# Batched 64x64 matmul: a gate before the second a tile's loads, its transposes behind the first multiplication, and two result blocks of every other tile for VectorE

## The chip, the cores and the metric

One core of one Trainium2 chip. The time is the device time of a launch in us; where several runs were made, the median is given. Every timed run used here was in the fast state; the state of the two kernels of transfers, run once each, is unknown.

A ratio is the mean time of one kernel's fast runs over that of the kernel before in the same rounds on the same chip, so it is not quite the ratio of the medians quoted beside it.

## The reference

```python
def setup_inputs():
    return {"a": np.random.randn(1024, 64, 64).astype(np.float32),
            "b": np.random.randn(1024, 64, 64).astype(np.float32)}

def reference(a, b):
    return np.matmul(a, b).astype(np.float32)
```

Each of a, b and the output is 16.78 MB. The program must read 33.55 MB and write 16.78 MB; there is little arithmetic.

## The kernel before

a is worked on in 8 tiles (s) of 128 batches, b and the result in 16 tiles (t) of 64 batches. A tile of a after the first comes as three quarters that GpSimd's DMA casts to bf16 on the way, and one plain fp32 quarter from ScalarE's queue. It is regrouped, transposed on TensorE as packed pairs of bf16, copied from PSUM by ScalarE, and spread by VectorE into block-diagonal weights. b comes plain on the queues of SyncE and ScalarE in turn and is cast on chip. Results leave PSUM in eight blocks per tile and go out through GpSimd's queue.

b is read in runs of `u n` = 128 fp32 (512 bytes), plain quarters of a in runs of `v k` = 1024 fp32 (4 KB), and results are written in runs of `w n` = 256 fp32 (1 KB).

```python
    a_v = a.rearrange("(s g h) (mp v) k -> s h g mp (v k)", h=4, g=32, v=16)
    b_v = b.rearrange("(t g h) (kp u) n -> t (h kp) g (u n)", h=4, g=16, u=2)
    o_v = out.rearrange("(t gh x) (mo w) n -> t (x mo) gh (w n)", gh=8, x=8, w=4)
    ...
    def load_a(s):
        a_sb = a_pool.tile([128, 3, 16, 64], bf16, name="a_sb")
        for h in range(3):
            nc.gpsimd.dma_start(                     # casts fp32 to bf16
                out=a_sb[:, h, :, :].rearrange("p v k -> p (v k)"), in_=a_v[s, h])
        a_raw = a_pool.tile([128, 16, 64], fp32, name="a_raw")
        nc.scalar.dma_start(out=a_raw[:]..., in_=a_v[s, 3])

    def load_b(t):
        b_sb = b_pool.tile([128, 16, 128], fp32, name="b_sb")
        queue = nc.scalar if t % 2 else nc.sync
        queue.dma_start(out=b_sb[:], in_=b_v[t])
    ...
    # stores, in multiply(t)
            nc.gpsimd.dma_start(out=o_v[t, :, lo : lo + n, :], in_=o_sb[:, lo : lo + n]...)
    ...
    with tc.manual_schedule():
        load_first_a()                               # plain, SyncE and ScalarE
        for t in range(3):
            load_b(t)
        ... # memsets, load_a(1), load_a(2) on GpSimd without a wait
        regroup(0); transpose(0, 0); transpose(0, 1)
        load_b(3); spread(0); cast(0)
        regroup(1); load_a(A_AHEAD); transpose(1, 0)
        for t in range(n_t):
            ... # spread(t+1), cast(t+1), load_b(t+4), load_a, multiply(t),
            ... # regroup(s+2), transposes, store(t-1)
```

(Cut; calls on one line are joined here.)

## Time and profile before

| | before |
|---|---|
| time, median of the first 3 runs (lowest, highest) | 135.2 us (134.85, 135.22) |
| span of the profiled run | 133.2 us |
| VectorE, ScalarE busy | 96.3, 86.8 us |
| first multiplication starts | 25.9 us |
| b0 landed, last b (b15) landed | 19.8, 113.7 us |
| last result copy ends, last store landed | 128.2, 131.7 us |

The prediction shows how these are read. One thing to keep in mind: GB/s in these views counts the written side, so a casting load counts half of what it reads.

### The profile page before, as it was taken

Reading aid. Unit: us, or ns where it says so; the run is one execution under the profiler, and the core shown is the slowest. Engines: PE = TensorE matmul, PEld = TensorE weight load, DVE = VectorE, ACT = ScalarE, POOL = GpSimd, SP = SyncE. Lnnn points to the kernel's source line nnn. Section 1 sums busy time; section 2 is a strip of 40 time slices with the busy share of each in tenths; the row PEclk is TensorE's granted clock in tenths of the full one; section 3 lists DMA queues with packets and bytes.
Section 4 is the critical chain, followed back from the end, with each engine's and each line's share of the span. In section 5 each row is a group of like instructions: output and inputs, shape, how many; then the busy total and the mean of one; then the engine's idle time right before and its main releaser. Section 6 shows DMA issues by size and latency. Waiting matters only on the chain.

```text
span 133.2 us, 2835 instructions
## 1 busy us (share of the span) xinstructions
PE 67.9 (51%) x1152; PEld 62.6 (47%) x1152; DVE 96.3 (72%) x121; ACT 86.8 (65%) x160; POOL 35.9 (27%) x49
## 2 busy tenths in 40 slices
PE   0000900784539259486358637951996195269300
PEld 0000900784439257475257527941995094268200
DVE  5920064943999249996999899799969996897740
ACT  3105525089950699489939992998399759969910
POOL 8981004000802017112413302030203020322460
PEclk9999995589965865579977985698569959955955
DMA  3999999999999999999999999999999999999893
GB/s 75 365 335 310 308 308 328 318 304 306 314 328 341 389 321 318 336 400 386 367 307 294 394 404 387 323 302 335 399 394 396 387 397 402 400 404 388 298 320 133
DMA packets 17485, 45.01 MB, mean 338 GB/s; under 512 B 1088, under 2 KB 1088, under 8 KB 17472
## 3 DMA queue, kind: packets, MB, share of 16 engines
q0 software_dynamic: 7440, 22.28, 54.7%
q10 hardware_dynamic: 5520, 13.11, 25.6%
q1 hardware_dynamic: 4512, 9.44, 20.1%
q8 instruction: 9, 0.15, 0.4%
q14 instruction: 4, 0.03, 0.1%
HBM read 33.55 MB, written 16.78 MB: 378 GB/s over the span
## 4 chain that ended last, share of the span: by engine, by line
DVE 29%; ACT 18%; PE 15%; DMA 13%; issue 10%; ACTq 7%; POOL 3%; SPq 1%; POOLq 1%; DVEq 0%
ACT o_sb L172 16%; DVE at_bd L128 14%; PE o_ps L184 13%; DMA b_sb<-in_b_dram 13%; DVE b_bf L139 6%; ACTq L72 4%; DVE o_sb L172 4%; POOL out_dram L161 3%; ACTq L91 3%; DVE a_bf L106 3%; PE at_ps L115 2%; DVE a_bf L103 2%; ACT b_bf L139 1%; SPq L85 1%; POOLq L274 1%
## 5 line engine op out<-in xcount | busy, mean ns | idle before, releaser
L172 ACT COPY o_sb<-o_ps 64x512 f32<-64x512 f32 x105 | 60.9, 580 | 20.3 <-PE o_ps L184 13.1
L184 PEld LDWEIGHTS <-at_bd 128*128 128x128 bf16 x1024 | 43.9, 115 | 35.5 <-DVE b_bf L139 25.1
L184 PE MATMUL o_ps<-b_bf,at_bd 128*128 128x64 bf16 x960 | 43.7, 218 | 31.2 <-DVE b_bf L139 22.4
L128 DVE COPY at_bd<-at_sb 32x1024 f32<-32x1024 f32 x64 | 45.6, 713 | 9.5 <-ACT at_sb L118 7.7
L161 POOL DMA_DIRECT2D out_dram<-o_sb x20 | 19.4, 968 | 77.9 <-DVE o_sb L172 72.5
L115 PE MATMUL at_ps<-identity,a_bf 128*128 128x128 f32 x128 | 23.3, 344 | 25.0 <-ACT a_bf L100 13.3
L115 PEld LDWEIGHTS at_ps<-identity,a_bf 128*128 128x128 f32 x128 | 19.3, 181 | 26.1 <-issue 20.8
L118 ACT COPY at_sb<-at_ps 128x512 f32<-128x512 f32 x32 | 17.4, 588 | 7.7 <-PE at_ps L115 7.3
L172 DVE COPY o_sb<-o_ps 64x512 f32<-64x512 f32 x15 | 10.4, 695 | 15.4 <-ACT o_sb L172 15.2
L139 DVE CAST b_bf<-b_sb 128x2048 bf16<-128x2048 f32 x14 | 17.4, 1245 | 0.4
L68 POOL DMA_DIRECT2D a_sb<-in_a_dram x21 | 12.5, 609 | 14.7 <-DVE a_bf L103 9.5
L106 DVE CAST a_bf<-a_raw 128x1024 bf16<-128x1024 f32 x7 | 7.0, 1003 | 1.9 <-DMA a_raw<-in_a_dram 1.9
L103 DVE COPY a_bf<-a_sb 128x3072 bf16<-128x3072 bf16 x7 | 6.7, 960 | 0.2
L100 ACT CAST a_bf<-o_sb 128x1024 bf16<-128x1024 f32 x2 | 2.0, 1042 | 7.4 <-issue 7.4
L100 DVE CAST a_bf<-o_sb 128x1024 bf16<-128x1024 f32 x2 | 2.5, 1228 | 2.6 <-DMA o_sb<-in_a_dram 2.6
L212 DVE MEMSET at_bd<- 128x4096 f32 x1 | 3.5, 3472 | 0.8 <-issue 0.8
L172 DVE COPY o_sb<-at_ps 64x256 f32<-64x256 f32 x8 | 3.4, 422 | 0.1
L139 ACT CAST b_bf<-b_sb 128x2048 bf16<-128x2048 f32 x1 | 1.9, 1898 | 2.3 <-DMA b_sb<-in_b_dram 2.3
L172 ACT COPY o_sb<-at_ps 64x256 f32<-64x256 f32 x8 | 2.9, 366 | 0.1
L209 ACT ACT_TABLE_LOAD x1 | 1.3, 1283 | 2.3 <-issue 2.3
L184 PE MATMUL at_ps<-b_bf,at_bd 128*128 128x64 bf16 x64 | 2.6, 212 | 0.3 <-DVE at_bd L128 0.3
L216 POOL MEMSET at_bd<- 128x2048 f32 x1 | 1.9, 1851 | 0.0
(12 smaller groups left out, 5.3 us busy)
## 6 DMA issues: line engine op xcount, KB each, us to landing
out_dram<-o_sb POOLq DMA_DIRECT2D x14, 1024.0 KB, 21.4
a_sb<-in_a_dram POOLq DMA_DIRECT2D x21, 256.0 KB, 19.7
a_raw<-in_a_dram ACTq DMA_DIRECT2D x7, 512.0 KB, 16.5
o_sb<-in_a_dram ACTq DMA_DIRECT2D x2, 512.0 KB, 7.3
o_sb<-in_a_dram SPq DMA_DIRECT2D x2, 512.0 KB, 6.4
out_dram<-o_sb POOLq DMA_DIRECT2D x2, 512.0 KB, 4.8
out_dram<-o_sb POOLq DMA_DIRECT2D x4, 256.0 KB, 3.7
b_sb<-in_b_dram SPq DMA_DIRECT2D x8, 0.5 KB, 16.8
```

The lines of the kernel that those rows point to most:

```text
L68: nc.gpsimd.dma_start(out=a_sb[:, h, :, :].rearrange("p v k -> p (v k)"), in_=a_v[s, h])
L72: nc.scalar.dma_start(out=a_raw[:].rearrange("p v k -> p (v k)"), in_=a_v[s, 3])
L100: copy(a_bf[:, :, h, :], a_sb[h].rearrange("p (v k) -> p v k", v=16))
L103: nc.vector.tensor_copy(a_bf[:, :, 0:3, :], cast_sb[:].rearrange("p h v k -> p v h k"))
L106: nc.vector.tensor_copy(a_bf[:, :, 3, :], raw[:])
L115: nc.tensor.transpose(at_ps[:, vo, :], a_cols[:, 4 * vo + 2 * j + wl, :], identity[:])
L118: nc.scalar.copy(at_tiles[s][:, j, :, wl, :, :], at_ps[:].rearrange("p vo (g mp) -> p g mp vo", mp=4),)
L128: nc.vector.tensor_copy(bd[rows, :, :, :, h, :].rearrange("p j g wl mo -> p j (g wl) mo"), at_tiles[t // 2][rows, :, half, :, :, :].rearrange(
L139: (nc.vector.tensor_copy if t else nc.scalar.copy)(b_bf[:], b_sb[:])
L161: nc.gpsimd.dma_start(out=o_v[t, :, lo : lo + n, :], in_=o_sb[:, lo : lo + n].rearrange("p gh j wl n -> p (gh j wl n)"),)
L172: copies[2 * par + wl](dst, src)
L184: nc.tensor.matmul(o_ps[:, gl, g % 2, j, :], at_bd[:, j, g, :, u], b_bf[:, g, 64 * u : 64 * u + 64], start=(u == 0), stop=(u == 1),)
```

## The change

Its intent: let b0, which the first multiplication needs, land without the casting loads of later a tiles in its way; let the first multiplication start without waiting for tile 1; and take VectorE's wait for ScalarE out of the even tiles.

```diff
@@ result blocks, in multiply(t)
                 copies = [nc.scalar.copy] * 4
-                if half:
-                    copies[3] = nc.vector.tensor_copy
+                if half and t % 2:
+                    copies[2:] = [nc.vector.tensor_copy] * 2
@@ before the loop
-        nc.gpsimd.memset(bd_tiles[1][:, 0], 0.0)
-        load_a(1)
-        nc.gpsimd.memset(bd_tiles[1][:, 1], 0.0)
-        for s in range(2, A_AHEAD):
+        nc.gpsimd.memset(bd_tiles[1][:], 0.0)
+        nc.gpsimd.tensor_copy(gate[:], a_tiles[0][3][:, 0:1])
+        for s in range(1, A_AHEAD):
             load_a(s)
...
-        regroup(1)
-        load_a(A_AHEAD)
-        transpose(1, 0)
@@ in the loop
-            if half == 0:
-                if s + 1 + A_AHEAD < n_s:
-                    load_a(s + 1 + A_AHEAD)
+            if half == 0 and 0 < s < n_s - 1 - A_AHEAD:
+                load_a(s + 1 + A_AHEAD)
             multiply(t)
-            if half == 0 and s + 2 < n_s:
+            if t == 0:
+                regroup(1)
+                load_a(A_AHEAD)
+                load_a(A_AHEAD + 1)
+                transpose(1, 0)
+            elif t == 1:
+                regroup(2)
+            elif half == 0 and s + 2 < n_s:
                 regroup(s + 2)
```

(The declaration of `gate` is left out.)

More of the change, by code (lines that the diff above doesn't have):

```diff
@@ L60 @@
     warm = consts.tile([128, 2], fp32)
+    gate = consts.tile([128, 1], fp32)
     a_tiles, b_tiles, abf_tiles, at_tiles, bbf_tiles = {}, {}, {}, {}, {}
```

## The prediction

> **What bounds the kernel now.** I read the page first. Its engine shares point at VectorE (72% busy), and its chain of waits is a mixture of VectorE, ScalarE and PE. Both mislead. The DMA row says that the 16 engines are full from the second slice to the last but one:
>
> ```profile
> span 133.2 us, 2835 instructions
> DVE  5920064943999249996999899799969996897740
> ACT  3105525089950699489939992998399759969910
> DMA  3999999999999999999999999999999999999893
> HBM read 33.55 MB, written 16.78 MB: 378 GB/s over the span
> ```
>
> To see whether "full" means "can do no more", I asked for busy time by stretch (columns: window, length, busy time of each engine, clock, DMA share, GB/s).
>
> ```profile
> 2.00:4.00 2.00, 0.00 (x0) 0.00 (x0) 2.00 (x1) 1.48 (x3) 2.00 (x3) 1.00 0.86 209
> 4.00:7.00 3.00, 0.00 (x0) 0.00 (x0) 2.79 (x2) 0.00 (x0) 3.00 (x4) 1.00 1.01 399
> 100.00:120.00 20.00, 10.92 (x217) 10.11 (x217) 17.98 (x23) 16.08 (x30) 4.24 (x4) 0.82 1.03 398
> 120.00:125.00 5.00, 4.07 (x91) 3.79 (x88) 3.36 (x7) 4.87 (x10) 0.83 (x2) 0.70 1.00 374
> 125.00:130.00 5.00, 0.00 (x0) 0.00 (x0) 3.04 (x8) 1.88 (x6) 3.53 (x5) 0.65 0.85 293
> ```
>
> A share stays above 1 only while queues are full (packets of several queues overlap on an engine). It is below 1 in two places: the first 4 us, and after 120 us, where the rate falls from 398 to 374 and 293 GB/s although stores are still to come.
>
> Next I priced the traffic, from DMA views of short windows (queue, packets, MB, share). The first line is the whole of 115 to 120 us, where only stores run. The next three are 102 to 110 us, stores with b. The last three are 10 to 15 us, casting loads of a (q0) beside two queues of b and plain a.
>
> ```profile
> q0 software_dynamic: 522, 2.01, 101.9%
> ...
> q0 software_dynamic: 469, 1.81, 58.7%
> q10 hardware_dynamic: 393, 0.80, 26.8%
> q1 hardware_dynamic: 267, 0.51, 16.9%
> ...
> q0 software_dynamic: 261, 0.47, 49.8%
> q1 hardware_dynamic: 261, 0.53, 30.9%
> q10 hardware_dynamic: 261, 0.53, 27.4%
> ```
>
> Stores: 2.01 MB in 5 us, 401 GB/s. b: in 8 us, 1.81 MB of stores take 4.5 us at that rate, so 1.33 MB of b (the window's 3.14 MB less the stores) go in 3.5 us, 381 GB/s. Casts: the two hardware queues' 1.07 MB take 2.8 us at that rate, so 0.47 MB written take the other 2.2 us, 215 GB/s of bf16 written. Plain a: 399 GB/s from the 4-to-7 us row. Now the whole program: stores 16.78 MB / 401 = 41.8 us; b 16.78 / 381 = 44.0; plain a, 11 loads of 0.524 MB, 5.77 / 399 = 14.5; casts, 21 loads of 0.262 MB, 5.51 / 215 = 25.6; instruction fetches about 0.6. Sum **126.5 us of full-rate DMA** in a span of 133.2. The rest is 6.7 us: 2.1 us before the first packet and about 1.0 in the half-filled start (2 to 4 us at 209 of 399 GB/s), some 1.8 from the last packet (131.4) to the end of the span, and the remaining 1.8 almost all after 120 us. Between 4 and 120 us nothing is lost.
>
> The tail of the issue list shows why the end is thin: the last stores land 3.3 to 7.0 us after issue, against a median of 17 over the kernel, so from tile 13 on the queue holds little and each store waits for its copies.
>
> ```profile
> 118.81 0.89 POOL L161 DMA_DIRECT2D out_dram<-o_sb  x1 [3.50 <-DVE o_sb L172]
> 122.42 0.76 POOL L161 DMA_DIRECT2D out_dram<-o_sb  x1 [2.72 <-ACT o_sb L172]
> 124.93 1.50 POOL L161 DMA_DIRECT2D out_dram<-o_sb  x2 [1.75 <-DVE o_sb L172]
> 128.45 0.72 POOL L161 DMA_DIRECT2D out_dram<-o_sb  x1 [0.34 <-DVE o_sb L172]
> ```
>
> So computation matters only in that it must finish early enough for the last stores to queue behind one another. It finishes at 127.7 us (last result copy) now, and at 25.9 us begins its first multiplication:
>
> ```profile
> 11.21 1.99 ACT L100 CAST a_bf<-o_sb 128x1024 bf16<-128x1024 f32 x2 [7.41 <-issue]
> 17.60 2.83 DVE L128 COPY at_bd<-at_sb 32x1024 f32<-32x1024 f32 x4 [7.33 <-ACT at_sb L118]
> 19.84 1.90 ACT L139 CAST b_bf<-b_sb 128x2048 bf16<-128x2048 f32 x1 [2.27 <-DMA b_sb<-in_b_dram]
> 25.88 0.32 PE L184 MATMUL o_ps<-b_bf,at_bd 128*128 128x64 bf16 x2
> ```
>
> **What the Trainium skill says.** "DMA: Bandwidth & Descriptors", section "Queues, rings and completion order", has each engine go round-robin between its queues by packet. The trace agrees: 261, 261 and 261 packets of three queues in 10 to 15 us. So a casting load holds b0 back even though it was issued later. The same page, section "Issuing engines are not separate DMA queues", says that DMAs of all issuers share the same 16 engines. That is why holding one queue back reorders the traffic and does not shorten it; the flat loss from 4 to 120 us agrees. The same page's "Specifications" gives about 358 GB/s of HBM per core; here stores run at 401, so the measurement decides. "VectorE: DVE Perf Modes", section "The TRN2 errata", has a PSUM copy cost VectorE 120 + FD cycles at 0.96 GHz and ScalarE 172 + FD at 1.2 GHz, 658 and 570 ns for 512 columns; the trace has 695 and 580.
>
> **The change, part by part.**
>
> *The gate.* GpSimd copies one column of the first a tile's last quarter before it issues the six casting loads of tiles 1 and 2 (and three of tile 3, next in its stream). That quarter lands at 9.99 us now. The casts put their first packets on at 7.1 us; without them in the way, I estimate 9.0 to 9.3. The first cast now took 3.5 us from the end of its issue to its first packet, so casts start near 12.7 us. From 9.0 to 12.7, b0 and b1 share the engines: 3.7 us at 381 GB/s is 1.41 MB, 0.70 each. The other 0.34 MB of each runs in a three-way round at 0.106 MB/us per queue (0.53 MB in 5 us), 3.2 us. b0 lands at **16.0** instead of 19.8. Bytes removed: none. Risk of an empty engine from 4 to 12.7: small, since 2.1 MB of first a and 2.1 MB of b are queued, 5.3 + 5.5 us of work.
>
> *Transposes and tile 1's loads behind the first multiplication.* ScalarE's first casts follow the a quarter by 1.2 us (9.99 to 11.21), so 10.3; the transposes and their copies take to 17.57 from 11.21, so 16.6; spread 2.8 us more, 19.4. b0's cast needs 1.9 us after 16.6 plus 0.7 for one load issue: 19.2. The first multiplication starts at about **19.4, 6.5 us earlier**: it no longer stands behind tile 1's transposes (which wait for tile 1 at 23.3), nor behind ScalarE's issue of a raw quarter, which blocked that engine from 19.84 to 27.0.
>
> *Result blocks.* Now VectorE takes one of eight in 15 tiles (15 x 695 ns); after, two of eight in seven odd tiles (14). ScalarE goes from 105 to 106. Busy time: nothing. What moves is VectorE's wait: it idles 15.2 us in 8 even tiles for ScalarE's copies of the same tile, about 1.0 us in each settled pair. Even tiles no longer have that wait, so I expect a pair to take 12.0 to 12.4 us instead of 12.6 to 12.8 where loads allow.
>
> *Sum for computation.* 6.5 us at the start and up to 0.5 x 7 later would finish it 6 to 10 us earlier. Loads will not let it have all: a tile 7 lands at 93.8 and is regrouped at 100.2, 6.4 us of slack. So 4 to 7 us: the last copy near **121 to 123**.
>
> *Sum for the time.* The end is 3.1 us of head + 126.5 of work + about 0.5 for the last stores not ending together = 130.1 for the last packet, against 131.4. That is 1.3 us, less whatever small hole the gate opens. I take **1.2 us**. The unprofiled time of 135.2 stands 2.0 over the span and should stay so: 135.2 - 1.2 = **134.0 us**, 0.9% faster.
>
> **Rivals.** *Computation is the bound (chain of waits, VectorE 72%):* then 6.5 us plus the shorter pairs come off the end, some 127 us. Against it: between 4 and 120 us no DMA engine has a free moment, so computation that runs sooner only lengthens the store queue. To reach 127 the traffic would need to be done in less than its 126.5 us. *The gate starves the engines:* two hardware queues of b alone are not seen in this trace, and GpSimd's casts start late. If 3.7 us ran at 80%, 0.7 us would be lost, leaving 134.7; a casting stream that then holds up tile 2 or 3 could use up the rest, 135.2. *Loads hold computation back:* a tiles 1 to 3 come some 4 us later, and stores queued earlier stand ahead of later a loads in the same queue. Then computation ends as now, the tail stays thin: 135.0. *A dearer mix:* if earlier stores beside casts cost more per packet, it would be slower than 136; the flat loss over very different mixes speaks against it.
>
> **Range and chances.** The floor with no tail loss at all is 3.1 + 126.5 + 1.8 + 2.0 = 133.4 us; to be faster by over 2% needs 132.5, below that floor and reachable only if my rates are 1% off or the head shrinks. I give it 0.05. Slower than 137.9 needs 2.7 us of new holes: 0.03. Range **133.0 to 135.3**.
>
> **What would show it.** First multiplication near 19.4 us; b0 landing near 16; casts' first packet near 12 to 13; DMA share unbroken between 4 and 125 us; the last result copy near 122; GB/s of the last slices near 400 until just before the end; last stores landing 6 us or more after issue; last packet near 130.1. I am wrong if the span falls below 131 (then DMA was not the bound, or its traffic got cheaper), or if a hole shows in the DMA row at 9 to 13 us, or if VectorE or PE waits for a tiles 2 and 3 so long that the tail is as thin as before.

## The result, and the profile after

The change made the kernel slower: 138.38 us (138.25 to 138.71) against 135.17 us, ratio 1.0247 (95% interval 1.0223 to 1.027). The profiled span grew from 133.2 to 136.5 us, by 3.3. Predicted were 134.0 us and 133.0 to 135.3.

The page of the kernel after: span, the DMA row and its rate in 40 slices, and the first line of its chain of waits.

```profile
span 136.5 us, 2833 instructions
...
DMA  3999999999999999999999999999999999999991
GB/s 80 386 351 291 299 329 319 304 308 313 320 303 305 304 378 359 291 326 398 392 383 326 310 342 393 385 355 302 318 384 397 405 408 403 348 359 329 322 318 42
...
DMA 62%; ACT 9%; issue 8%; POOL 5%; PE 4%; DVE 4%; ACTq 1%; POOLq 1%; DVEq 0%
```

The DMA row has no hole at all: it is as full as before, and longer. The chain is now 62% DMA, where before it went mostly through the engines. The loss is in the rate, and at both ends. The same windows by stretch (columns as in the prediction; DMA share and GB/s are the last two), first before, then after:

```profile
9.00:14.00 5.00, 0.70 (x4) 0.73 (x5) 0.69 (x1) 1.99 (x2) 0.95 (x2) 1.00 1.07 305
...
116.00:120.00 4.00, 2.17 (x41) 2.17 (x42) 3.88 (x5) 2.78 (x6) 0.89 (x1) 0.53 1.03 406
...
124.00:128.00 4.00, 0.32 (x12) 0.20 (x7) 3.86 (x9) 2.86 (x8) 2.77 (x4) 0.81 0.84 294
```

```profile
9.00:14.00 5.00, 1.88 (x9) 1.91 (x10) 0.41 (x1) 2.58 (x3) 4.59 (x9) 1.00 1.06 291
...
112.00:116.00 4.00, 2.00 (x64) 1.88 (x64) 1.99 (x3) 3.93 (x8) 1.29 (x1) 1.00 1.03 401
116.00:120.00 4.00, 1.65 (x32) 1.65 (x32) 3.86 (x6) 2.36 (x5) 0.00 (x0) 0.59 1.01 354
120.00:124.00 4.00, 3.05 (x58) 2.89 (x56) 3.79 (x6) 3.64 (x7) 2.11 (x2) 0.50 0.99 340
124.00:128.00 4.00, 2.50 (x47) 2.33 (x44) 3.06 (x8) 3.87 (x10) 1.92 (x3) 0.63 1.01 333
128.00:132.00 4.00, 0.00 (x0) 0.00 (x0) 0.31 (x1) 0.07 (x1) 1.67 (x3) 0.80 0.99 326
```

**The head.** The two rows of 9 to 14 us look alike, 305 and 291 GB/s at shares of 1.07 and 1.06, and are not. The DMA view of 10 to 14 us in the kernel after has two queues, b0 and b1 alone:

```profile
DMA packets 569, 1.17 MB, mean 291 GB/s; under 512 B 0, under 2 KB 0, under 8 KB 569
...
q10 hardware_dynamic: 285, 0.58, 53.3%
q1 hardware_dynamic: 284, 0.58, 53.1%
```

In the same 4 us the kernel before moved 1.24 MB, of which 0.37 MB were written by casting loads and so read as 0.74: 1.61 MB read, 403 GB/s, against 291. Counted in the same way (DMA views of 0 to 20 us), the kernel before had read 5.67 + 1.18 = 6.85 MB by 20 us and the kernel after 5.77 + 0.47 = 6.24: 0.61 MB less, at 403 GB/s about **1.5 us**. (Priced with the prediction's rates, the packets by 16 us give about 1.3 us, from 3.0 to 4.3 us of lost work; the 1.4 and the 4.5 in the expectations below are an earlier count of this.)

**The tail.** In the kernel after, the last load's packets end at 108.2 us (before: 113.1), and 9.0 MB of stores (6.5) are left. They go at 400 GB/s for 8 us and then at 326 to 354, although the queue is full: its last nine stores all land 6.0 us or more after their issue (before, the last landed 3.3 us after).

**Computation.** Its early part went as predicted: b0 landed at 16.3 us, the first multiplication started at 19.4. But it was held up later, as the waits of VectorE in the kernel after show; the second line is the regrouping of tile 7:

```profile
DVE a_bf L104 <- DMA a_sb<-in_a_dram: 8.6, 3, 6.8
...
100.54 0.96 DVE L104 COPY a_bf<-a_sb 128x3072 bf16<-128x3072 bf16 x1 [6.81 <-DMA a_sb<-in_a_dram]
```

Tile 7's casts landed at 100.5 us instead of 93.8, behind earlier stores in GpSimd's queue. The last result copy ended at 128.3 us, where it had ended before.

### The profile page after: what moved, and what is told of

Same layout as the page of the kernel before. It is cut to its first block, busy times and chain, and to the rows that moved or that the text cites. A ratio compares the mean times of both kernels' runs of the same rounds, so it can differ in the third digit from the quotient of the medians.

```text
span 136.5 us, 2833 instructions
## 1 busy us (share of the span) xinstructions
PE 67.2 (49%) x1152; PEld 62.7 (46%) x1152; DVE 92.8 (68%) x120; ACT 88.0 (64%) x161; POOL 38.2 (28%) x49
## 4 chain that ended last, share of the span: by engine, by line
DMA 62%; ACT 9%; issue 8%; POOL 5%; PE 4%; DVE 4%; ACTq 1%; POOLq 1%; DVEq 0%
DMA a_sb<-in_a_dram 37%; DMA out_dram<-o_sb 20%; ACT o_sb L173 7%; DMA o_sb<-in_a_dram 6%; POOL out_dram L162 3%; PE o_ps L185 3%; POOL a_sb L69 2%; DVE at_bd L129 2%; PE at_ps L116 1%; DVE a_bf L107 1%; DVE b_bf L140 1%; ACT at_sb L119 1%; ACT b_bf L147 1%; ACTq L92 1%; POOLq L278 1%
## 5 line engine op out<-in xcount | busy, mean ns | idle before, releaser
L185 PE MATMUL o_ps<-b_bf,at_bd 128*128 128x64 bf16 x960 | 42.0, 215 | 30.2 <-DVE b_bf L140 23.8
L162 POOL DMA_DIRECT2D out_dram<-o_sb x20 | 20.1, 1005 | 51.0 <-DVE o_sb L173 14.2
L116 PEld LDWEIGHTS at_ps<-identity,a_bf 128*128 128x128 f32 x128 | 20.0, 185 | 28.6 <-issue 21.3
L69 POOL DMA_DIRECT2D a_sb<-in_a_dram x21 | 13.9, 680 | 35.3 <-DVE a_bf L104 13.0
L173 DVE COPY o_sb<-o_ps 64x512 f32<-64x512 f32 x14 | 9.6, 689 | 0.6 <-ACT o_sb L173 0.3
L107 DVE CAST a_bf<-a_raw 128x1024 bf16<-128x1024 f32 x7 | 5.5, 790 | 0.0
L185 PE MATMUL at_ps<-b_bf,at_bd 128*128 128x64 bf16 x64 | 3.6, 242 | 1.0 <-DVE at_bd L129 1.0
L215 POOL MEMSET at_bd<- 128x4096 f32 x1 | 3.5, 3508 | 0.0
L101 DVE CAST a_bf<-o_sb 128x1024 bf16<-128x1024 f32 x2 | 1.4, 678 | 3.0 <-DMA o_sb<-in_a_dram 3.0
## 6 DMA issues: line engine op xcount, KB each, us to landing
a_raw<-in_a_dram ACTq DMA_DIRECT2D x7, 512.0 KB, 14.5
```

The costliest lines, as they stand in the source:

```text
L69: nc.gpsimd.dma_start(out=a_sb[:, h, :, :].rearrange("p v k -> p (v k)"), in_=a_v[s, h])
L107: nc.vector.tensor_copy(a_bf[:, :, 3, :], raw[:])
L116: nc.tensor.transpose(at_ps[:, vo, :], a_cols[:, 4 * vo + 2 * j + wl, :], identity[:])
L173: copies[2 * par + wl](dst, src)
L185: nc.tensor.matmul(o_ps[:, gl, g % 2, j, :], at_bd[:, j, g, :, u], b_bf[:, g, 64 * u : 64 * u + 64], start=(u == 0), stop=(u == 1),)
L215: nc.gpsimd.memset(bd_tiles[1][:], 0.0)
```

## The experiments

The theory formed from the traces: (1) b loads alone run slow, so the gate, which leaves b alone with itself, loses work at the head; (2) stores alone run slow once the loads are some 8 us gone, so every us by which stores are pushed behind the last load is paid back at a worse rate. The rivals: computation waits for later a tiles; the result blocks; the new order.

### Each part alone

The gate alone on the kernel before:

```diff
-        nc.gpsimd.memset(bd_tiles[1][:, 0], 0.0)
-        load_a(1)
-        nc.gpsimd.memset(bd_tiles[1][:, 1], 0.0)
-        for s in range(2, A_AHEAD):
+        nc.gpsimd.memset(bd_tiles[1][:], 0.0)
+        nc.gpsimd.tensor_copy(gate[:], a_tiles[0][3][:, 0:1])
+        for s in range(1, A_AHEAD):
```

> The kernel before with the gate alone: GpSimd's casting loads wait for the last quarter of the first a tile; order of transposes and result blocks as before. Theory (two queues of b alone run at some 290 GB/s instead of 381, and stores alone sink to some 325 GB/s about 8 us after the last load): the hole at 9 to 14.5 us appears here in full, +1.4 us of lost DMA work by 16 us, little change of the tail: about 136.6 us, ratio 1.010. Rival (computation waits for later a tiles, DMA is not what is lost): the DMA work by 16 us is as before, the loss comes from a later end of computation. Rival (the result blocks did it): ratio 1.000.

Measured: 137.93 us (before 134.99), ratio 1.0212 (1.0197 to 1.0227). Nearly the whole loss; more than the 1.010 expected, because the tail got worse too. Computation was not late here: the last result copy ended at 127.2 us (before: 128.2), and the last nine stores landed 7.3 us or more after their issue. Its rows:

```profile
9.00:14.00 5.00, 1.51 (x7) 1.54 (x8) 0.60 (x1) 2.38 (x3) 4.28 (x9) 1.00 1.06 291
...
124.00:128.00 4.00, 0.00 (x0) 0.00 (x0) 3.06 (x8) 1.91 (x6) 3.36 (x5) 0.81 1.00 323
128.00:132.00 4.00, 0.00 (x0) 0.00 (x0) 0.00 (x0) 0.00 (x0) 0.18 (x1) 0.50 0.98 326
```

The result blocks alone on the kernel before:

```diff
-                if half:
-                    copies[3] = nc.vector.tensor_copy
+                if half and t % 2:
+                    copies[2:] = [nc.vector.tensor_copy] * 2
```

> The kernel before with the result blocks alone (VectorE takes two of eight in odd tiles, none in even ones). Theory: no loss at the head; computation frees buffers a little sooner, loads end up to 2 us sooner, the stores-only stretch grows by as much: 135.2 to 135.8 us, ratio 1.000 to 1.004. Rival (the result blocks did it): +3 us, ratio 1.02.

Measured: 135.18 us, ratio 1.0022 (1.0001 to 1.0044). The blocks do not cost the time. Computation did end 2.7 us sooner (last copy 125.5 us against 128.2), and nothing came of it.

The kernel after without the gate:

```diff
-        nc.gpsimd.memset(bd_tiles[1][:], 0.0)
-        nc.gpsimd.tensor_copy(gate[:], a_tiles[0][3][:, 0:1])
-        for s in range(1, A_AHEAD):
+        nc.gpsimd.memset(bd_tiles[1][:, 0], 0.0)
+        load_a(1)
+        nc.gpsimd.memset(bd_tiles[1][:, 1], 0.0)
+        for s in range(2, A_AHEAD):
             load_a(s)
```

> The kernel after without the gate: memsets and casting loads as before, the first multiplication ahead of tile 1's transposes, result blocks as after. Theory: no hole at 9 to 14.5 us; first multiplication near 22 us; loads end some 3 us sooner than before, so the stores-only stretch is that much longer and costs about 0.6 us: 135.8 us, ratio 1.004. Rival (an earlier start shortens the program, as was predicted): 134.0, ratio 0.992. Rival (order and blocks did it): 138, ratio 1.02.

Measured: 135.33 us, ratio 1.0022 (1.001 to 1.0035). The first multiplication started at 20.9 us, 5 us sooner, and the end was not sooner. Its last stores were queued 7 us deep, and still the row of 124 to 128 us says 327 GB/s. So it was not a thin queue that made the end of this kernel slow.

The new order alone (as above, with the old result blocks):

> The kernel before with the new order alone (first multiplication ahead of tile 1's regrouping, transposes and the next a loads), without gate and with the old result blocks. Theory: like no_gate to within 0.4 us, 135.2 to 135.8 us, ratio 1.000 to 1.004. Rival (the new order lets a loads come late and holds computation back): 137 or more, ratio 1.013.

Measured: 135.34 us, ratio 1.0025 (1.0004 to 1.0047). Neutral (at most 0.5%).

A sum that comes within 0.7 us of all of these, always short (its 8 us and its rates were read from before and after): the end of the last store is the end of the last load, plus 8 us at 400 GB/s (3.2 MB), plus the remaining stores at 325 GB/s. Last load and stores left are taken from the DMA packets of each trace.

| kernel | last load ends | stores left | sum | last store's packet ends |
|---|---|---|---|---|
| before | 113.1 us | 6.46 MB | 131.1 us | 131.4 us |
| order alone | 112.9 | 6.50 | 131.1 | 131.1 |
| blocks alone | 111.7 | 6.98 | 131.3 | 131.8 |
| after without gate | 111.2 | 7.15 | 131.4 | 131.7 |
| gate alone | 111.1 | 7.98 | 133.8 | 134.4 |
| after | 108.2 | 8.99 | 134.0 | 134.7 |

Without a hole at the head, loads that end 1 us sooner leave about 0.4 MB more of stores, which then take 1.2 us: a loss of 0.2. The gate's hole leaves its lost work to the stores on top of that.

### The transfers by themselves

One kernel of transfers with waits between the stages (output wrong). Its core:

```python
for i in range(4):   # A: b_v rows of 512 B, both queues; B: SyncE's alone
    (nc.scalar if i % 2 else nc.sync).dma_start(out=y[i][:], in_=b_v[i])
# C, F: the same bytes, rows of 8 KB: b.rearrange("(t q) (y k) n -> t (q y) (k n)", q=64, y=2)
# D: b_v on SyncE's queue, rows of 8 KB on ScalarE's
for t in range(8):   # E: GpSimd's queue; G: SyncE's
    nc.gpsimd.dma_start(out=o_v[t], in_=x[:])
```

> Transfers by themselves, one stage after another with a wait between; the output is wrong on purpose. A: four b tiles as the kernel reads them (512-byte rows) on both hardware queues. B: the same on one. C: the same bytes as rows of 8 KB on both. D: two b tiles on one queue beside two a-like tiles in 8 KB rows on the other. E: eight 1 MB stores from GpSimd. F: four loads as C. G: eight stores from SyncE. Theory (two queues of 512-byte rows get in each other's way; stores alone sink whatever the queue): A near 290 GB/s, C near 400, D well over A; E begins near 400 and is near 325 from some 8 us (3 MB) on; G does the same again. Rival for the head (any two hardware queues without GpSimd's are slow): A and C both near 290. Rival for the tail (the software queue, or the addresses of the last tiles): E holds 400, or G does.

Measured, by stretch (columns: window, length, VectorE, ScalarE and GpSimd busy, clock, DMA share, GB/s); in order A, B, C, the end of D with b alone, E, F, G:

```profile
6.00:16.00 10.00, 0.00 (x0) 0.00 (x0) 0.00 (x0) 1.00 1.05 289
22.00:34.00 12.00, 0.00 (x0) 0.00 (x0) 0.00 (x0) 1.00 1.06 290
40.00:46.00 6.00, 0.00 (x0) 0.00 (x0) 0.00 (x0) 1.00 1.01 427
58.00:62.00 4.00, 0.14 (x1) 0.00 (x0) 0.00 (x0) 1.00 1.06 291
68.00:82.00 14.00, 0.00 (x0) 0.00 (x0) 3.17 (x4) 1.00 1.00 324
98.00:103.00 5.00, 0.00 (x0) 0.00 (x0) 0.00 (x0) 1.00 1.01 428
108.00:130.00 22.00, 0.00 (x0) 0.00 (x0) 0.00 (x0) 1.00 1.04 343
```

b in 512-byte rows alone makes 290 GB/s, on two queues or on one. So "two queues get in each other's way" was wrong in my expectation; it is this traffic alone. The share is the *highest* where the rate is lowest; in B a single queue has 1.06, so a share above 1 does not need packets of several queues, as the prediction had it. In D, b beside rows of 8 KB, the two together made 396 and 378 GB/s (52 to 54 and 54 to 56 us). Stores in 1 KB rows alone make 324 on GpSimd's queue and 343 on SyncE's, at once, without the 8 good us that I expected in E and G.

Where do those come from? A second kernel of transfers:

```python
# H: four stores, rows of 1 KB, from four tiles; I: three stores, rows of 8 KB
# J: nine stores, rows of 1 KB, begun together with two b tiles on both hardware queues
for i in range(2):
    (nc.scalar if i % 2 else nc.sync).dma_start(out=y[i][:], in_=b_v[i])
for t in range(9):
    nc.gpsimd.dma_start(out=o_v[7 + t], in_=x[t % 8][:])
```

> Stores by themselves; the output is wrong on purpose. H: four 1 MB stores from four tiles in the kernel's rows of 1 KB. I: three stores in rows of 8 KB. J: nine stores in rows of 1 KB, begun together with two b tiles, so that some 7 MB of stores go on alone afterwards. Theory (stores in rows of 1 KB alone are slow, and stores keep 400 GB/s for some 8 us after loads have gone by): H near 330 from the start, I above 400, J's stores 400 for about 8 us after the last b packet and near 330 from then on. Rival (it takes the kernel's own state at the end, whatever that is): J falls to 330 at once. Rival (writing itself is limited, whatever the rows): I near 330 too.

Measured; H, I, then three stretches of J: beside b, just after b's end (43.9 us), and later:

```profile
10.00:16.00 6.00, 5.09 (x3) 0.00 (x0) 0.60 (x1) 1.00 1.00 324
21.00:27.00 6.00, 0.00 (x0) 0.00 (x0) 0.00 (x0) 1.00 1.02 415
36.00:42.00 6.00, 0.00 (x0) 0.00 (x0) 0.89 (x1) 1.00 1.03 396
44.00:48.00 4.00, 0.00 (x0) 0.00 (x0) 0.00 (x0) 1.00 1.03 406
52.00:60.00 8.00, 0.00 (x0) 0.00 (x0) 0.00 (x0) 1.00 1.01 334
```

Stores in 8 KB rows alone are fast, in 1 KB rows alone slow, and 1 KB rows are fast beside loads and for some 4 us after them (8 us in the kernels). That reproduces the form of the kernels' tail. Company did not help at once, though: in J's first stretch, 32 to 36 us, stores and b together made only 325 to 332 GB/s, and 399 from 36 us on. So in J the rate followed the company with a delay of some 4 us at both ends. Why is not shown by any run here.

### Taking the slow traffic out of both kernels

The main test: the same two kernels with longer rows in memory. The results land in wrong places; tiles, bytes, queues and waits are the same.

```diff
+    o_w = out.rearrange("(t h q) (y k) n -> t (q y) h (k n)", h=2, q=32, y=4)     # long stores: 4 KB
...
-            nc.gpsimd.dma_start(out=o_v[t, :, lo : lo + n, :], in_=...)
+            nc.gpsimd.dma_start(out=o_w[t], in_=src.rearrange("p (h e) -> p h e", h=2))
...
-    b_v = b.rearrange("(t g h) (kp u) n -> t (h kp) g (u n)", h=4, g=16, u=2)
+    b_v = b.rearrange("(t h q) (y k) n -> t (q y) h (k n)", h=4, q=16, y=8)         # long b: 2 KB
```

(The partial stores of the last tiles are cut; they write 2 or 4 KB rows.)

> The kernel before with every store writing rows of 4 KB instead of 1 KB: same tiles, sizes, queue and waits, result in the wrong places on purpose. Theory: stores alone no longer sink, so the last 11 us run at some 400 GB/s: 133.4 us, ratio 0.987. Rival (the end is thin because computation is late): 135, ratio 1.000.

> The kernel after with the same stores in rows of 4 KB, wrong on purpose. Theory: its 19 us of slow stores run at some 400 GB/s, so it gains about 3.3 us, more than the kernel before does: 135.2 us, and stands some 1.7 us over before_long_stores, which is the hole at the head alone. Rival (the tail is not what makes the change slow): the distance to the kernel before with long stores stays at 3.3 us.

> The kernel before with stores in rows of 4 KB and b loads in rows of 2 KB instead of 512 bytes, wrong on purpose. Theory: all traffic near 400 GB/s, 132 us, ratio 0.977.

> The kernel after with both. Theory: neither hole nor slow tail is left, so what was predicted of the change holds here: within 0.7 us of before_long_both, on either side. Rival (something else in the change costs time too): 1.5 us or more over it.

> The kernel before with b loads in rows of 2 KB alone, stores in rows of 1 KB as they were, wrong on purpose. The slow end is left. b comes a little sooner, so loads end sooner and the slow end grows; a small hole of the longer rows' own near 10 us: 135 to 136 us.

> The kernel after with the same b loads, wrong on purpose. Theory: the distance of the pair is what the slow end alone makes, 3.3 less the 1.9 left with long stores: 1.0 to 1.8 us. Rival (the hole and the slow end are not separate, one needs the other): below 0.5 or still 3 us.

Measured, medians of 4 runs each (ratio to the unchanged kernel before of the same rounds, whose medians were 134.95 to 135.22 us):

| | before | after | distance |
|---|---|---|---|
| as they are | 135.2 us | 138.4 us (1.0247) | 3.2 us |
| long stores | 134.3 (0.993) | 136.2 (1.0058) | 1.9 |
| long b | 134.6 (0.9964) | 135.9 (1.006) | 1.3 |
| both | 134.0 (0.9903) | 134.0 (0.991) | 0.0 |

(The first row's pair ran in earlier rounds than the others.) The distances add up: taking the slow stores away takes 1.3 us, the slow b 1.9, both all of it. Within the noise (each time is good to some 0.4 us), the loss goes with these two kinds of traffic. In the windows of after with long stores, the head's 291 GB/s is still there and the rates of 326 to 354 of the tail are gone; with both, both are:

```profile
9.00:14.00 5.00, 1.57 (x8) 1.61 (x9) 0.44 (x1) 2.44 (x3) 4.39 (x9) 1.00 1.06 291
116.00:124.00 8.00, 4.95 (x90) 4.80 (x91) 7.12 (x11) 6.25 (x12) 1.61 (x2) 0.60 0.99 399
```

```profile
9.00:14.00 5.00, 3.51 (x16) 3.27 (x16) 0.52 (x1) 2.80 (x4) 4.60 (x9) 1.00 1.00 358
116.00:124.00 8.00, 6.74 (x128) 6.33 (x128) 6.58 (x13) 6.63 (x14) 2.25 (x3) 0.57 0.98 392
```

Four reservations.

- Longer b rows open a hole of their own at 8 to 12 us in both kernels (212 GB/s at a share of 0.85 in 10 to 12 us of before with both, 215 at 0.76 in 9 to 10 us of after with both), which I did not explain. It does not make the distance: by 20 us both had read 6.6 MB (the kernel before as it is: 6.85).
- With long stores the end of the kernel after is thin: its last result copy ended at 128.1 us (before with long stores: 124.5), its last stores landed 3.1 to 3.5 us after issue, and the DMA share was 0.81 at 126 to 128 us. So late computation may have a part in the 1.9 us. Most of it is the head: 0.72 MB less read by 20 us, 1.8 us at 403 GB/s.
- Longer rows also lie in other places. The rows that one partition reads of a b tile are 64 KB apart with 512 bytes and 256 KB apart with 2 KB; for the stores it is 128 KB with 1 KB and 512 KB with 4 KB; and rows of 8 KB follow on from each other. No run separates length from spacing, so "short rows" means rows laid out as here.
- Absolute times missed their expectations by up to 2 us (134.0 instead of 132 for before with both; 134.3 for before with long stores lies halfway between the theory's 133.4 and the rival's 135). So the rows' gain in the kernels is smaller than the rates alone say.

### Attempts to mend it

ScalarE's plain a quarters ahead of b1, so that b0 has other company while the casts are held back (correct result):

```diff
-        for t in range(3):
-            load_b(t)
+        load_b(0)
+        for s in range(1, A_AHEAD):
+            raw_tiles[s] = load_raw(s)      # the plain quarter of load_a(s), moved here
+        for t in range(1, 3):
+            load_b(t)
```

> The kernel after, gate and all, with one difference: ScalarE issues the plain quarters of a tiles 1 and 2 (rows of 4 KB) before b1, so that b0 has plain a beside it while the casts are held back, and not b1. Same bytes, same gate. Theory: the hole at 8 to 15 us closes (lost DMA work by 20 us 3.0 instead of 4.5), and the end comes some 1.5 x 401 / 325 = 1.8 us sooner or a little more: 136.0 to 136.5 us, ratio 1.008 to 1.011. Rival (late casting loads, not the hole, cost the time): 138 as after, ratio 1.02.

Measured: 137.41 us, ratio 1.0173 (1.0148 to 1.0197): 1.0 us better than after, less than expected. The head closed by half only (344 GB/s in 9 to 14 us; 6.57 MB read by 20 us, against 6.24 in after and 6.85 in before), and its tail is as long as after's (last load 107.7 us, 8.9 MB of stores left).

Four attempts at the tail all failed. Stores of even tiles on SyncE's queue:

```diff
-            nc.gpsimd.dma_start(
+            (nc.gpsimd if t % 2 else nc.sync).dma_start(
                 out=o_v[t, :, lo : lo + n, :],
```

> The kernel before with the stores of even tiles issued by SyncE instead of GpSimd, so that they share a queue with b loads and get a larger part of the round. Theory: stores move forward, loads end later, the stores-only stretch at the end is shorter than 18 us and loses less: 134.0 us, ratio 0.992, unless computation then waits for loads and holes open. Rival (the end is thin because computation is late): 135, ratio 1.000.

Measured: 144.87 us, ratio 1.0722. VectorE then waits 11.9 us for b tiles, and 80 to 120 us ran at 337 to 346 GB/s. Why it ran at that is open.

Three b buffers instead of four (`B_AHEAD = 3`):

> The kernel before with three b buffers instead of four: b loads are issued one tile later, so loads end later and stores come forward. Theory: the stores-only stretch shrinks from 18 to some 15 us, 134.6 us, ratio 0.996, if computation still finds its b tiles (they landed 15 to 20 us after issue, and a pair takes 12.6 us, so it may wait a little). Rival (prefetch is what keeps the program fast): 136 or more, ratio 1.008.

Measured: 145.84 us, ratio 1.0782. The rival was nearer, and far too mild: the DMA share fell to 0.90 at 92 to 96 us and to 0.67 to 0.83 between 124 and 136 us, and the last load ended at 124.4 us.

After without gate, and four result buffers instead of eight (`bufs=4`):

> The kernel after without the gate and with four result buffers instead of eight: computation has 4 to 5 us to spare there and now waits for stores to land, so b buffers come free later and the last load ends later. Theory: for each us that the last load ends later the end comes some 0.2 us sooner, as long as computation still ends before 127 us: 134.7 us, ratio 0.997. Rival (computation loses more than it had to spare): 136 or more, ratio 1.007.

Measured: 141.53 us, ratio 1.0472. The last load ended at 117.8 us as wanted, but the DMA share then fell to 0.80 at 116 to 124 us and 0.13 at 124 to 128: computation did not have the 4 to 5 us to spare that I took it to have.

Useless reads beside the last stores:

```diff
+            if t == 13:
+                nc.vector.memset(spare[:, 0:1], 0.0)
+                for i in range(8):          # 6 in the kernel before
+                    nc.sync.dma_start(out=spare[:], in_=<128 KB of b in rows of 1 KB>)
             multiply(t)
```

> The kernel after with useless traffic added: from tile 13 on, eight loads of 128 KB, one after another, into a spare tile, while only stores are left. 1.05 MB more to move, 2.5 us at full rate. Theory (stores are slow because they are alone): beside reads the stores go faster than 325 GB/s, so the time grows by clearly less than 2.5 us, or falls: 137.5 to 139.5 us, ratio 1.018 to 1.032, with the store rate beside the reads back at 380 or more of both directions together. Rival (the tail is bound by something else than the mix): +2.5 us or more, 141 us, ratio 1.043.

> The same addition to the kernel before: six loads of 128 KB from tile 13 on, 0.79 MB, 1.9 us at full rate. Theory: part of the last 11 us of slow stores runs faster, so +1 us at most: 135 to 136 us, ratio 1.000 to 1.007. Rival: +1.9 us or more, 137, ratio 1.014.

Measured: 150.14 us (1.1112) and 142.58 us (1.0553). Inconclusive: each read waited for the one before it, and most of them ran after the last store. They lengthened the program by themselves and say nothing on the stores.

No kernel that I ran with a correct result beats the kernel before.

## Why the prediction was wrong

**The step that failed** is "Sum for the time": 3.1 us of head + 126.5 us of work + about 0.5. The work term was mis-sized in two places, because each rate was taken from windows where that traffic had company, or had had it shortly before. The last packet ended at 134.7 us, not 130.1. Of these 4.6 us about 1.5 are the head; for the tail I estimate 3.4 (the stores left at 108.2 us less 3.2 MB are 5.8 MB, at 325 instead of 401 GB/s), together 4.9.

- *The gate, "3.7 us at 381 GB/s" and "risk of an empty engine: small".* The engines were not empty. b alone runs at 290 GB/s, and it was alone from about 8.6 to 14.5 us, since the first cast's packet came at 14.6, not 12.7 (the prediction's 9.2 + 3.5 leaves out the 0.7 us of the issue, and 3.5 from its end became 4.4). The estimate 5.9 us x (1 - 290/381) = 1.4 us agrees with the 1.5 counted. The rival "the gate starves the engines" had the mechanism in sight and sized it at 0.7 us.
- *The tail, "the queue holds little and each store waits for its copies".* The end of the kernel before was thin (share 0.84 at 124 to 128 us), but filling it gained nothing: in the kernel after without the gate, the queue was 7 us deep and the rate was still 327 GB/s. Stores in 1 KB rows alone run at 324 to 343. There was about 1.3 us to gain at the end only if stores ran at 401 to the last; they do not, and more of them at the end cost more. (The 127.7 us that the prediction gives for the last result copy is where that copy begins; it ended at 128.2.)
- *"The floor" of 133.4 us* fell with the same rates. It was no floor for the change, and the range was too narrow above: it took the rates to be good to 1%, where the traffic's company moves them by 15 to 24% (stores from 401 to 324 or 343 GB/s, b from 381 to 290). The rival "a dearer mix" looked for a dear price beside casts; the dear prices were those of b and of stores alone, so "the flat loss over very different mixes" did not speak against them.

**What was right.** DMA is the bound, and the rival "computation is the bound" (127 us) fell: 5 to 6.5 us of earlier start moved nothing. b0's landing (16.0 predicted, 16.3) came out by luck in part: b ran slower than reckoned, but the casts also came 1.9 us later. The first multiplication (19.4, 19.4) and the settled pair (12.0 to 12.4; SyncE's b loads, one per pair, were issued 12.2, 11.6 and 12.6 us apart from 52 to 88 us) came out, the latter with its reason: VectorE's wait for ScalarE's result copies fell from 15.2 to 0.3 us. The rival "loads hold computation back" came true as well: the last copy ended at 128.3 us, not 121 to 123. In the kernel after it does not show in the time, since the queue stayed full (stores landed 6.0 us or more after issue); where stores are quick it may cost a little (second reservation above).

**What in the profile could have told.** I read the DMA share: above 1 is full, so nothing is lost. The Trainium skill, "Perfetto Trace Analysis", section "Identifying the Most-Contended Engine", says to go by HBM utilization for DMA, since 16 engines make occupancy misleading. The runs agree: share 1.06 at 290 GB/s, 1.01 at 427. And the trace of before had the clue: its 120 to 125 us ran at 374 GB/s with a share of 1.00, which a thin queue does not explain.

The change gains 3.2 us more from longer rows (distance 3.2 to 0.0) than before does, so what it loses is bound to this layout in memory. A cause deeper than "this traffic alone is slow" (what in the memory or the engines does it) stays open.

## What to carry to other kernels

When DMA is the bound, a change that reorders transfers is not neutral: traffic that runs at full rate beside other traffic may lose 15 to 24% of it when it is left alone, as b in rows of 512 bytes did behind the gate (381 to 290 GB/s) and stores in rows of 1 KB by themselves (401 to 324 or 343). Take a transfer's price from a stretch with the same company as it will have after the change, or measure it by itself; and judge a stretch by bytes per us, counted on the side that is read where loads cast, not by the busy share.

## What the Trainium skill lacked or had wrong

- "DMA: Bandwidth & Descriptors", section "Specifications", gives 512 bytes as the least transfer for line rate. Here loads in rows of 512 bytes (64 KB apart) alone made 289 to 291 GB/s, loads of the same size in rows of 8 KB 427 to 428.
- The same section's row of about 358 GB/s of HBM per core (a stack's 716 over two cores) did not bind: with this program on one core, loads made 427 GB/s and stores 415 in 8 KB rows. It is no contradiction, as the prediction took it to be: the same page's section "Bandwidth" has 425 GB/s at 16 MB for one core, and 358 for both cores of a pair at work.
- No page has the rate of stores in short rows: 1 KB rows alone 324 GB/s (GpSimd's queue) or 343 (SyncE's), 8 KB rows 415.
- No page says that such traffic can run at full rate beside other traffic, nor that stores keep it for 4 to 8 us afterwards: 396 beside b (after 4 us at 325 to 332), 406 just after, 334 later.
- No page warns that the busy share of the DMA engines can rise as the rate falls (1.06 at 290 GB/s, 1.01 at 427); "Perfetto Trace Analysis" only says that occupancy misleads.
